# Staging tiles ordered by last use, and a norm started behind the recurrence's last channel

## The chip, the cores and the metric

The kernel runs on one core of one Trainium2 chip. The metric is the device time of one execution in microseconds (us). The core has five engines with an instruction queue each: PE (TensorE, matmuls into PSUM; its weight loads are listed as PEld), DVE (VectorE), ACT (ScalarE), POOL (GpSimd) and SP (SyncE, which here only issues DMAs). Each engine runs its instructions in the order in which they stand; an instruction waits on semaphores of other engines and of DMA queues.

## The reference

Two layers of an encoder, for 2048 prompt frames and 32 further frames of a second request; feature size 1024. Layer 0 is attention (a sliding window branch and a band branch), layer 1 a gated linear recurrence. Each is wrapped in two RMS norms:

```python
hp = rms_norm(yp, ln_pre[l])
...                                   # layer 0
qa, ka, va, ga, qb, kb, vb, gb = ab_project(hp, pos_p, w_in_ab[j])
oa = prompt_band(qa, ka, va, N_PREV_A, None, sinks_a[j])
ob = prompt_band(qb, kb, vb, N_PREV_B, relpos_b[j], None)
mp = concat(oa * silu(ga), ob * silu(gb)) @ w_out
...                                   # layer 1, lru_mixer
xb, z = split(h @ w_in)
xc = conv_b + sum(xp[:, tap:tap + t] * conv_w[tap] for tap in range(4))
r  = sigmoid(xr @ wa + ba);  gi = sigmoid(xr @ wx + bx)
a  = exp(8 * r * log_sigmoid(lam))
u  = sqrt(1 - a * a) * (gi * xc)
h[t] = a[t] * h[t-1] + u[t]
mp = (h * silu(z)) @ w_out
...                                   # both
yp = yp + rms_norm(mp, ln_post[l])
```

The outputs are the two activations, the new key and value caches and the recurrence's states. All is float32.

## The kernel before

**Tiling.** Features lie on the 128 partitions in 8 groups (KT), frames on the free axis. The 2084 frames are cut into six blocks of 352 (the last 324), and worked on in three *thirds* (b = 0, 1, 2) of two blocks (bi = 0, 1). A float32 product is made of three matmuls of a rounded format: every operand is split into a high and a low part (r0h/r0l and r1h/r1l are the two activation tiles, wh/wl the weights), so a block of one result tile is 8 x 3 = 24 matmuls into one PSUM tile (acc, of which there are three from layer 0's out projection on).

**Stages.** Layer 0's in projection for all thirds (`dense_P`) with attention between; then layer 0's out projection of the three thirds (`out_part`); then, for each third, layer 1's in projection with the recurrence (`in_part`, 16 result tiles) and its out projection (`out_part`, 8 result tiles). `dense_2` holds the last two.

**What sets the order.** All engines' instructions are recorded through one helper (line 106 in every profile row), in the order that a small planner (`Sched`) makes: processes are generators that ask for an engine, inputs and buffers; the planner keeps model times and issues from the list by priority. The order is fixed when the program is built; on the chip each engine then keeps it, whatever the true times are. A key set by `sch.set` exists only in the planner. So a process that waits for a key is recorded later, and the chip knows nothing of the key.

**The staging pool and the pool that takes its place.** `sp` (named stg, right side of the memory) holds what layer 0's in projection needs to bring its results out: `s` (seven tiles of 352, the result before it is stored; the gates z are stored from here to `zT` last of all), `sr` (high and low parts), `vst` (transposed values), `xcs` (cosines and sines), `r0b` (a norm's factor). It is closed when layer 0's in projection is recorded, and `mp` takes the same memory: `m` (two tiles of 8 x 352, the out projection's result), `sacc` (sums of squares), `r`, `tz`. Tiles are laid out in the order in which they are made. `reuse_waits="tile"` makes the first write of a tile in `mp` wait for the last use of the tiles that lay in the same place, DMAs that read them included. In `out_part` the first result of a block makes ACT write `m` and `sacc` (`fin_out`, `c == 0`).

**Layer 1.** For a channel group c, `in_part` makes the x branch (`fin_x`): convolution, gates (g, two PSUM tiles, from xs), ACT functions on e and ti, then on DVE `e`, `ti`, the scan over time (the profile's TENSOR_TENSOR_SCAN, `ti<-ex,hcar,ti`), the product with the gate z (ex from tzb), and the split into r0h and r0l. At its end the key `("yc", b, c)` is set. The names ex and eti are tiles that several uses share: ex holds xc, a and sz, and xt at other times; eti holds e or ti.

`out_part` is called with `late=True`: its first two blocks run 21 matmuls each, over the first seven channel groups, and only then the three matmuls each over the eighth, which wait for `("yc", b, 7)`.

**The norm of the next third.** `norm_proc` for third b + 1 is spawned when `in_part` of third b begins. It loads the first block's two halves xt from `x2T`, then for each block: four squares on ACT (sq, one buffer), each followed by a reduction on DVE (ss), their sum, a split into xs, two matmuls with ones on PE (`misc<-xs,onesr`), a square root, reciprocals, products (xt), and the split into r1h and r1l, which the next in projection reads. The second block is loaded into the same tiles when the first is done. With `hold` the process waits for a key before its first square; before, this is `("part", b)`, set when `in_part` of third b has recorded its last matmul.

`sch.alone` keeps POOL out of the choice between DVE and POOL while `in_part` is being recorded; it is set to False when `in_part` ends.

Of the kernel before, what the change touches and what calls it, by code (L numbers as in the profile page):

```python
# [9 lines left out]
F32 = mybir.dt.float32  # L10
F32R = mybir.dt.float32r
# [5 lines left out]
KT = 8  # L17
# [5 lines left out]
BLK = 352  # L23
# [25 lines left out]
PY2, PY3 = 0.5, 3  # L49
# [121 lines left out]
class Sched:  # L171
# [119 lines left out]
    def spawn(self, gen, prio):  # L291
        self.n += 1
        p = [prio, self.n, gen, None]
        p[3] = next(gen, None)
        if p[3] is not None:
            self.procs.append(p)
            self.procs.sort(key=lambda q: (q[0], q[1]))
# [106 lines left out]
def hybrid_kernel(ctx, tc, I, O):  # L404
    nc = tc.nc
    sch = Sched()
# [14 lines left out]
    def ring(pool, shape, tag, bufs, dtype=F32):  # L421
        return Ring(sch, pool, shape, dtype, tag, bufs)
# [189 lines left out]
    hlr = []  # L612
# [131 lines left out]
    r0, fx = [rr_.get(), None], {}  # L744
# [110 lines left out]
    sp = PS.enter_context(tc.tile_pool(name="stg", bufs=1, side="right"))  # L855
# [6 lines left out]
    pS = P.enter_context(tc.tile_pool(name="pS", bufs=1, space=bass.MemoryType.PSUM))  # L862
    pT = P.enter_context(tc.tile_pool(name="pT", bufs=1, space=bass.MemoryType.PSUM))
    pO = P.enter_context(tc.tile_pool(name="pO", bufs=1, space=bass.MemoryType.PSUM))
    sr = ring(sp, [128, BLK], "s", 7)
    srr = ring(sp, [128, 2, BLK], "sr", 3, F32R)
    hlr.append(srr)
    vsr = ring(sp, [128, 3, 2, 128], "vst", 1, F32R)

    xcr = ring(sp, [128, KT, 176], "xcs", 1)  # L870
    xct = {}
    ctn = {}
    r0[1] = sp.tile([128, BLK], F32, name="r0b", tag="r0b")

    def ct_done(b, c):
        n, t = ctn.get((b, c), (0, 0.0))
# [756 lines left out]
    Q = ctx.enter_context(ExitStack())  # L1633
    mp = Q.enter_context(tc.tile_pool(name="mp", bufs=1, side="right", reuse_waits="tile"))
    ac3 = accr
    mr, sar, r2r = ring(mp, [128, KT, BLK], "m", 2), ring(mp, [128, BLK], "sacc", 2), ring(mp, [128, BLK], "r", 1)
    tzr = ring(mp, [128, BLK], "tz", 1)
    sch.cuts.update((x[2].tensor.name, (KT * BLK, BLK // 2)) for x in mr.idle)
    x2n = {}
    gr = []  # L1640
# [214 lines left out]
    def gw_proc():  # L1855

        for b in range(3):
            for c in range(8):
                g, = yield R("SP", rings=[gstr])
                SP.dma_start(out=g, in_=I["gw"][c])  # L1860
                e, (gh, gl) = yield R(("A", "V"), [g], [ghr, glr], cost=(0.3, 0.2))
                if e == "A":
                    A.copy(gh, g)
                else:
                    V.tensor_copy(gh, g)
                e, _ = yield R(("V", "G"), [gh], cost=(0.33, 0.69))
                ENG[e].tensor_tensor(gl, g, f32(gh), OP.subtract)
                gws[(b, c)] = gh, gl
                gstr.release(g)
                sch.set(("gw", b, c), sch.t[e] + 0.13)  # L1870
# [149 lines left out]
    def dense_2():  # L2020
        for b in range(3):
            yield from out_part(b, base + 8 * b, b % 2, I["xT"], LN_POST, x2T, lambda k, bi, b=b: (("y", b), bi), late_m=b > 0)
            if b == 0:

                yield R("PE", [("attention",)])
        spawn(gw_proc(), 1)
        xrr.retire(eti)
        for x in extra:
            xtr.retire(x)
        b1 = base + 24  # L2030
        for b in range(3):
            sch.alone = True
            if b < 2:
                spawn(norm_proc(x2T, b + 1, LN_PRE + 1, 1, (1, b + 1), [xtr, xtr], free=("in", b), src_ready=[("x2", b + 1)],
                                hold=("part", b)), PY3)
            yield from in_part(b, b1 + 24 * b, 1, 0)
            sch.alone = False
            sch.set(("part", b))
            yield from out_part(b, b1 + 24 * b + 16, 0, x2T, LN_POST + 1, O["yT"], lambda k, bi, b=b: ("yc", b, k), late=True, final=b == 2)

    spawn(dense_2(), 9)
    sch.run(lambda: not names() & {"kq_proc", "v_proc", "proc", "reduce"})
    P.close()
# [149 lines left out]
```

## Time and profile before

| what | value |
|---|---|
| median of 3 runs | 1810.09 us (1809.11 to 1812.69) |
| the profiled execution: time, span | 1810.39 us, 1808.6 us |
| PE busy, share of the span | 1726.3 us, 95% |
| DVE, ACT, POOL busy | 1537.9, 1001.9, 322.1 us |
| layer 0's out projection, first third | about 985 to 1053 us |
| layer 1, in projection of the three thirds | 1179 to 1323, 1394 to 1531, 1599 to 1730 us |
| layer 1, out projection of the three thirds | 1323 to 1394, 1531 to 1599, 1730 to 1795 us |

A row of a timeline reads: start in us from the span's start, length in us, engine, line, operation, output <- inputs, shapes, and in brackets how long the engine had been idle and what ended that. A row of stretches gives start and end, length, then for each engine its busy us and the number of instructions, then the granted clock of PE (PEclk, 1.00 is full), the share of time that the DMA engines worked, and GB/s.

### The profile page before, as it was taken

The page shows a single profiled execution, that of the slowest core. Times are in us where ns is not written, and L with a number is a line of the kernel's source. Part 1 is how long each engine was busy: PE and PEld are TensorE (multiplying, and loading weights), DVE is VectorE, ACT ScalarE, POOL GpSimd, SP SyncE. Part 2 cuts the span into 40 slices and gives each one's busy share as a digit, 9 for nine tenths or more (in the row PEclk, how much of TensorE's full clock was granted, in tenths as well). Part 3 has the DMA queues.
Part 4 walks back from the last instruction along what each step waited for, and adds up shares of the span by engine and source line. Part 5 has one row for each costly group of instructions (what it writes and reads, how often), then busy time and mean ns, then how long its engine had stood idle before and what let it go on. Part 6 is the DMA issues. An engine that isn't in the chain of part 4 may idle for free. (4 is left out here: it accounts for less than half of the span.)

```text
span 1808.6 us, 31683 instructions
## 1 busy us (share of the span) xinstructions
PE 1726.3 (95%) x11078; PEld 1674.2 (93%) x11078; DVE 1537.9 (85%) x3228; ACT 1001.9 (55%) x2055; POOL 322.1 (18%) x285
## 2 busy tenths in 40 slices
PE   8998999999999999999997999998989999999997
PEld 7988999898899999899997999998989999999996
DVE  9889977799998769998888689999988998789945
ACT  4275543367766525766664334457754587438742
POOL 4332123322312133323124000000012000100002
PEclk9999999999999999999999999999999999999998
DMA  5787766879565268887875864674556634455466
GB/s 180 204 256 235 227 183 180 225 218 276 161 188 153 73 182 244 209 229 195 226 192 163 274 211 169 233 295 160 207 182 222 246 124 143 162 208 172 146 242 232
DMA packets 232168, 362.80 MB, mean 201 GB/s; under 512 B 36340, under 2 KB 173480, under 8 KB 231992
## 3 DMA queue, kind: packets, MB, share of 16 engines
q1 hardware_dynamic: 232008, 360.78, 64.0%
q8 instruction: 87, 1.43, 0.3%
q14 instruction: 73, 0.60, 0.1%
HBM read 255.77 MB, written 107.00 MB: 201 GB/s over the span
## 5 line engine op out<-in xcount | busy, mean ns | idle before, releaser
L106 PE MATMUL acc<-r0h,wh 128*128 128x352 f32 (+2 forms) x1832 | 592.8, 324 | 11.5 <-ACT r0h L106 10.3
L106 PE MATMUL acc<-r0l,wh 128*128 128x352 f32 (+2 forms) x1832 | 593.1, 324 | 2.1 <-DVE r0l L106 2.0
L106 PE MATMUL acc<-r0h,wl 128*128 128x352 f32 (+2 forms) x1832 | 592.6, 323 | 2.3 <-DMA wl<-wo1s 1.6
L106 PEld LDWEIGHTS acc<-r0h,wh 128*128 128x128 f32 x1832 | 347.1, 189 | 14.0 <-ACT r0h L106 11.2
L106 PEld LDWEIGHTS acc<-r0l,wh 128*128 128x128 f32 x1832 | 347.1, 189 | 4.4 <-DVE r0l L106 3.4
L106 PEld LDWEIGHTS acc<-r0h,wl 128*128 128x128 f32 x1832 | 347.0, 189 | 4.3 <-DMA wl<-wo1s 2.4
L106 PE MATMUL acc<-r1h,wh 128*128 128x352 f32 (+1 forms) x864 | 277.9, 322 | 0.6 <-ACT xb L106 0.6
L106 PE MATMUL acc<-r1h,wl 128*128 128x352 f32 (+1 forms) x864 | 277.7, 321 | 0.0
L106 PE MATMUL acc<-r1l,wh 128*128 128x352 f32 (+1 forms) x864 | 277.6, 321 | 0.0
L106 ACT ACTIVATE pt<-pt,nm 128x256 f32<-128x256 f32 (+6 forms) x272 | 170.3, 629 | 70.0 <-DVE nm L106 68.9
L106 ACT CAST pp<-T 128x256 fp32r<-128x256 f32 (+4 forms) x314 | 133.1, 439 | 74.2 <-PE T L106 62.2
L106 POOL TENSOR_SCALAR pt<-pt,rr 128x256 f32<-128x256 f32 (+5 forms) x144 | 99.3, 699 | 397.5 <-DVE rr L106 183.4
L106 PEld LDWEIGHTS acc<-r1h,wh 128*128 128x128 f32 x864 | 162.7, 188 | 0.9 <-ACT xb L106 0.9
L106 PEld LDWEIGHTS acc<-r1l,wh 128*128 128x128 f32 x864 | 162.8, 188 | 0.0
L106 PEld LDWEIGHTS acc<-r1h,wl 128*128 128x128 f32 x864 | 162.6, 188 | 0.2 <-DVE wl L106 0.2
L106 DVE TENSOR_TENSOR pp<-T,pp 128x256 fp32r<-128x256 f32 (+4 forms) x314 | 151.3, 498 | 8.6 <-ACT pp L106 6.7
L106 PE MATMUL T<-ident,pt 128*128 128x128 f32 (+1 forms) x864 | 141.7, 274 | 15.5 <-DVE pp L106 12.5
L106 PE MATMUL O<-pp,vt 128*128 128x256 f32 (+2 forms) x728 | 133.8, 307 | 8.7 <-DVE pp L106 5.8
L106 PEld LDWEIGHTS T<-ident,pt 128*128 128x128 f32 (+1 forms) x864 | 100.2, 139 | 40.6 <-DVE pp L106 20.0
L106 ACT ACTIVATE m<-acc,vec 128x352 f32<-128x352 f32 (+3 forms) x103 | 51.1, 511 | 141.3 <-PE acc L106 135.6
L106 PE MATMUL S<-kk,qa 128*128 128x320 f32 (+5 forms) x376 | 121.5, 337 | 4.5 <-issue 1.5
L106 PEld LDWEIGHTS O<-pp,vt 128*128 128x128 f32 x728 | 104.5, 189 | 13.0 <-DVE pp L106 7.1
(243 smaller groups left out, 3051.6 us busy)
## 6 DMA issues: line engine op xcount, KB each, us to landing
wst<-w_in SPq DMA_DIRECT2D x93, 512.0 KB, 4.9
wst<-wo_in SPq DMA_DIRECT2D x32, 512.0 KB, 4.1
wh<-w1s SPq DMA_DIRECT2D x32, 512.0 KB, 3.6
wl<-w1s SPq DMA_DIRECT2D x32, 512.0 KB, 4.8
wh<-wo1s SPq DMA_DIRECT2D x24, 512.0 KB, 3.8
wl<-wo1s SPq DMA_DIRECT2D x24, 512.0 KB, 4.7
kk<-kB SPq DMA_DIRECT2D x32, 320.0 KB, 4.9
vt<-vB SPq DMA_DIRECT2D x16, 640.0 KB, 4.7
```

The costliest lines, as they stand in the source:

```text
L106: r = fn(*a, **k)
```

## The change

Three edits. The tiles of `sp` are made in the order r0b, vst, xcs, sr, s instead of s, sr, vst, xcs, r0b. The tiles of `mp` are made in the order sacc, r, tz, m instead of m, sacc, r, tz. The next third's norm waits for `("yc", b, 7)`, whose model time is the end of the eighth channel's split, instead of `("part", b)`.

```diff
-    sr = ring(sp, [128, BLK], "s", 7)
+
+    r0[1] = sp.tile([128, BLK], F32, name="r0b", tag="r0b")
+    vsr = ring(sp, [128, 3, 2, 128], "vst", 1, F32R)
+
+    xcr = ring(sp, [128, KT, 176], "xcs", 1)
     srr = ring(sp, [128, 2, BLK], "sr", 3, F32R)
     hlr.append(srr)
-    vsr = ring(sp, [128, 3, 2, 128], "vst", 1, F32R)
-
-    xcr = ring(sp, [128, KT, 176], "xcs", 1)
+    sr = ring(sp, [128, BLK], "s", 7)
     xct = {}
     ctn = {}
-    r0[1] = sp.tile([128, BLK], F32, name="r0b", tag="r0b")
...
-    mr, sar, r2r = ring(mp, [128, KT, BLK], "m", 2), ring(mp, [128, BLK], "sacc", 2), ring(mp, [128, BLK], "r", 1)
+
+    sar, r2r = ring(mp, [128, BLK], "sacc", 2), ring(mp, [128, BLK], "r", 1)
     tzr = ring(mp, [128, BLK], "tz", 1)
+    mr = ring(mp, [128, KT, BLK], "m", 2)
...
                 spawn(norm_proc(x2T, b + 1, LN_PRE + 1, 1, (1, b + 1), [xtr, xtr], free=("in", b), src_ready=[("x2", b + 1)],
-                                hold=("part", b)), PY3)
+                                hold=("yc", b, KT - 1)), PY3)
             yield from in_part(b, b1 + 24 * b, 1, 0)
             sch.alone = False
-            sch.set(("part", b))
```

By bytes, the first `m` (bi = 0) lay over all seven `s` and the first `sr`, and lies now over `xcs` and `sr`; the second (bi = 1) lies now over `sr` and the seven `s`.

What the planner makes of it. Up to the end of layer 1's first in projection every engine has the same instructions in the same order; only waits differ. ACT's rows at the first result of layer 0's out projection, before (m is the result's tile, acc its PSUM tile, the numbers are buffers, and each DMAHW is a semaphore of DMA queues):

```order
L106 CAST r0h<-xr_153 128x4x176 [waits Pool_49]
L106 ACTIVATE m_10500<-acc_158,vec 128x2x176 [waits DMAHW2_49,DMAHW1_49,DMAHW3_49,DMAHW0_49,DMAHW6_49,DVE_49,PE_49]
L106 ACTIVATE sacc_10502<-acc_158 128x352
L106 CAST r0h<-xt_151 128x4x176 [waits DVE_49]
L106 CAST r0h<-xt_152 128x4x176 [waits DVE_49]
L106 CAST r1h<-ex_0_10570 128x4x176 [waits DMAHW4_49,DVE_49]
L106 CAST wh_119<-wst_118 128x1024 [waits DMAHW5_49,PE_49]
L106 ACTIVATE m_10501<-acc_0_10557,vec 128x2x176 [waits PE_49]
```

The same rows of ACT now:

```order
L106 CAST r0h<-xr_153 128x4x176 [waits Pool_49]
L106 ACTIVATE m_10504<-acc_158,vec 128x2x176 [waits DVE_49,PE_49]
L106 ACTIVATE sacc_10500<-acc_158 128x352
L106 CAST r0h<-xt_151 128x4x176 [waits DVE_49]
L106 CAST r0h<-xt_152 128x4x176 [waits DVE_49]
L106 CAST r1h<-ex_0_10570 128x4x176 [waits DMAHW2_49,DMAHW3_49,DMAHW1_49,DMAHW4_49,DMAHW0_49,DVE_49]
L106 CAST wh_119<-wst_118 128x1024 [waits DMAHW5_49,PE_49]
L106 ACTIVATE m_10505<-acc_0_10557,vec 128x2x176 [waits DMAHW2_49,DMAHW3_49,DMAHW1_49,DMAHW6_49,DMAHW0_49,PE_49]
```

Nothing moved; the waits on DMAs went from the first m to the r1h cast and the second m.

DVE at the end of layer 1's first in projection, before. These are the eighth channel's e, ti, scan (here SCALAR_TENSOR_TENSOR `ti<-ex,hcar,ti`), the product with the gate, and r0l, with the norm's reductions (ss) and the out projection's weights (wl) among them:

```order
L106 SCALAR_TENSOR_TENSOR e_10562<-ex_0_10571,e_10562 128x704
L106 TENSOR_REDUCE ss_155<-sq_154 128x176
L106 TENSOR_TENSOR ti_10563<-ti_10563,e_10562 128x704
L106 TENSOR_TENSOR wl_122<-wst_117,wh_119 128x1024
L106 SCALAR_TENSOR_TENSOR ti_10563<-ex_0_10571,hcar,ti_10563 128x704
L106 COPY hcar<-ti_10563 128x1
L106 SCALAR_TENSOR_TENSOR ex_0_10571<-tzb_10558,acc_159 128x352
L106 TENSOR_REDUCE ss_156<-sq_154 128x176
L106 SCALAR_TENSOR_TENSOR ti_10563<-ti_10563,ex_0_10571 128x704
L106 TENSOR_REDUCE ss_155<-sq_154 128x176
L106 TENSOR_TENSOR r0l<-ti_10563,r0h 128x704
L106 TENSOR_REDUCE ss_156<-sq_154 128x176
```

The same place on DVE now:

```order
L106 SCALAR_TENSOR_TENSOR e_10562<-ex_0_10571,e_10562 128x704
L106 TENSOR_TENSOR ti_10563<-ti_10563,e_10562 128x704
L106 SCALAR_TENSOR_TENSOR ti_10563<-ex_0_10571,hcar,ti_10563 128x704
L106 COPY hcar<-ti_10563 128x1
L106 SCALAR_TENSOR_TENSOR ex_0_10571<-tzb_10558,acc_159 128x352
L106 SCALAR_TENSOR_TENSOR ti_10563<-ti_10563,ex_0_10571 128x704
L106 CAST r0h<-ti_10563 128x704
L106 TENSOR_TENSOR r0l<-ti_10563,r0h 128x704
L106 TENSOR_REDUCE ss_155<-sq_154 128x176
L106 CAST wh_120<-wst_118 128x1024
```

Three reductions moved behind r0l, the cast r0h came over from ACT, and wl went to POOL, whose rows from there on are, now:

```order
L106 TENSOR_TENSOR wl_124<-wst_117,wh_121 128x1024
L106 TENSOR_TENSOR wl_122<-wst_117,wh_119 128x1024
L106 TENSOR_TENSOR sacc_10501<-sacc_10501,tzb_10558 128x352
L106 TENSOR_TENSOR wl_122<-wst_118,wh_119 128x1024
L106 TENSOR_TENSOR sacc_10500<-sacc_10500,tz_10503 128x352
```

The second of these is the wl that moved; POOL's row ahead of it is from layer 0's out projection. On ACT the first square of this norm now stands behind the weights' cast and the gate's tzb, the others behind the evacuation of the first two blocks. On PE the norm's two matmuls (misc) stand 32 matmuls later.

DVE at the end of the second in projection, before:

```order
L106 TENSOR_TENSOR ti_10563<-ti_10563,e_10562 128x704
L106 TENSOR_REDUCE ss_155<-sq_154 128x176
L106 SCALAR_TENSOR_TENSOR ti_10563<-ex_0_10571,hcar,ti_10563 128x704
L106 COPY hcar<-ti_10563 128x1
L106 SCALAR_TENSOR_TENSOR ex_0_10571<-tzb_10558,acc_159 128x352
L106 TENSOR_REDUCE ss_156<-sq_154 128x176
L106 SCALAR_TENSOR_TENSOR ti_10563<-ti_10563,ex_0_10571 128x704
L106 TENSOR_REDUCE ss_155<-sq_154 128x176
L106 TENSOR_TENSOR r0l<-ti_10563,r0h 128x704
L106 TENSOR_REDUCE ss_156<-sq_154 128x176
```

And now:

```order
L106 TENSOR_TENSOR ti_10563<-ti_10563,e_10562 128x704
L106 SCALAR_TENSOR_TENSOR ti_10563<-ex_0_10571,hcar,ti_10563 128x704
L106 COPY hcar<-ti_10563 128x1
L106 SCALAR_TENSOR_TENSOR ex_0_10571<-tzb_10558,acc_159 128x352
L106 SCALAR_TENSOR_TENSOR ti_10563<-ti_10563,ex_0_10571 128x704
L106 CAST r0h<-ti_10563 128x704
L106 TENSOR_TENSOR r0l<-ti_10563,r0h 128x704
L106 TENSOR_REDUCE ss_155<-sq_154 128x176
```

Again the reductions moved behind r0l and the cast came to DVE; no weights are split in between. ACT has two of the four squares ahead of the first evacuation and two behind the second block's. On PE the norm's two matmuls stand 36 matmuls later, and the sum of the two ss halves (`ss<-ss,ss`) is on POOL. From there on the third in projection has its instructions in a somewhat different order: the gates' matmuls stand 8 to 16 matmuls later.

## The prediction

> **What bounds the kernel now.** I read the page first, then the waits of PE, then the time around its longest waits.
>
> ```profile
> span 1808.6 us, 31683 instructions
> ...
> PE 1726.3 (95%) x11078; PEld 1674.2 (93%) x11078; DVE 1537.9 (85%) x3228; ACT 1001.9 (55%) x2055; POOL 322.1 (18%) x285
> ```
>
> PE is the bound: only what shortens PE's stream or its waits shortens the kernel. The waits of PE, by what ended them (total us, times, longest):
>
> ```profile
> PE acc L106 <- ACT r0h L106: 10.3, 3, 4.6
> ...
> PE acc L106 <- DVE r0l L106: 2.0, 3, 1.0
> ```
>
> These six are three pairs at three places, which I call A (988 us: first result of layer 0's out projection), B0 and B1 (1330 and 1538 us: layer 1's out projection of the first and the second third, two blocks in, where the eighth channel is needed). In the stretches below, the columns are length, then busy us and instructions of PE, PEld, DVE and ACT, then PEclk, the granted clock.
>
> ```profile
> 984.80:988.01 3.21, 3.21 (x20) 2.92 (x19) 3.13 (x5) 0.65 (x1) 2.47 (x1) 1.00 0.94 282
> 988.01:992.62 4.61, 0.00 (x0) 0.00 (x1) 0.02 (x1) 1.57 (x3) 2.12 (x1) 0.94 0.55 139
> 992.62:998.94 6.32, 6.05 (x19) 5.68 (x20) 3.59 (x5) 1.56 (x2) 0.00 (x0) 0.51 1.02 309
> 1329.77:1333.83 4.06, 0.17 (x2) 0.00 (x0) 3.91 (x6) 1.52 (x2) 0.00 (x0) 0.94 0.71 234
> 1333.83:1340.35 6.52, 5.71 (x19) 5.34 (x19) 5.39 (x5) 2.96 (x6) 2.75 (x2) 0.51 0.20 79
> 1538.23:1540.22 1.99, 0.16 (x2) 0.00 (x0) 1.93 (x3) 1.57 (x2) 0.00 (x0) 1.00 0.00 0
> 1540.22:1545.17 4.95, 3.97 (x13) 3.73 (x14) 4.14 (x6) 3.33 (x6) 0.00 (x0) 0.66 0.20 16
> ```
>
> At full speed 20 matmuls take 3.21 us, 0.16 each. After each wait the clock is halved for some 3.4 or 6.8 us. So A costs 4.61 + 6.32 - 19 x 0.16 = 7.9 us; B0 costs 4.06 + 6.52 - 18 x 0.16 = 7.7 (18 begin in it); B1 costs 1.99 + 4.95 - 13 x 0.16 = 4.9. Together 20.5 us can be had. The rest of PE's waits the change leaves alone.
>
> **A: the tiles in another order.** The queue, ACT, DVE and POOL around 988 us; the first row is the issue line of the last store from a staging tile (median us to landing last).
>
> ```profile
> zT<-s SPq DMA_DIRECT2D x1, 162.0 KB, 5.3
> ...
> 985.44 0.46 SPq L106 DMA_DIRECT2D zT<-s  x1
> ...
> 985.54 4.60 POOL L106 TENSOR_TENSOR wl<-wst,wh 128x1024 fp32r<-128x1024 f32 x1 [3.68 <-DVE wh L106]
> ...
> 987.05 0.88 DVE L106 TENSOR_TENSOR xt<-xt 128x704 f32<-128x704 f32 x1
> ...
> 990.99 0.56 ACT L106 ACTIVATE m<-acc,vec 128x352 f32<-128x352 f32 x1 [5.54 <-DMA xt<-zT]
> 991.45 0.46 ACT L106 ACTIVATE sacc<-acc 128x352 f32<-128x352 f32 x1
> 991.79 0.78 ACT L106 CAST r0h<-xt 128x704 fp32r<-128x704 f32 x1
> ...
> 992.60 0.89 DVE L106 TENSOR_TENSOR r0l<-xt,r0h 128x704 fp32r<-128x704 f32 x1 [4.67 <-ACT r0h L106]
> ```
>
> The store is issued at 985.44 and lands 5.3 later, at 990.8 (the profile names another transfer of the same moment, the load xt<-zT; m waits for five DMA semaphores); m, whose tile lies over its source, is written at 990.99, 3 us after its matmuls ended (988.01). Behind m in ACT's order stands the r0h cast that PE waits for. In the changed order m's wait names no DMA any more; the first m lies over tiles last used earlier. Then m runs at 988.25 (0.25 for the signal, an estimate from 990.8 to 990.99), r0h 0.80 behind it, at 989.05, its input ready since 987.93; PE restarts at 989.9 instead of 992.62. The next step is late at once: r0l has to share with POOL, which works on wl until 990.13, so it ends at 991.05. The second piece (xt 0.88, r0h 0.78, r0l 0.89) ends at 993.55; before, PE at half clock hid it, now PE waits 0.8 us more for it. The 20 steps from the last matmul before the wait end at 994.55 instead of 998.94: 4.4 us. If the clock halves once, it is 3.3. I take 3.8. Ends: 2.0 (halved twice) and 5. The second m, which now lies over the late tiles, is written some 9 us later, after the store has landed: nothing. The r1h cast behind takes over the DMA waits, but is needed only 50 us later: nothing. The tiles' new places cost no instruction.
>
> **B0: the norm's squares behind the eighth channel.** ACT and DVE in the order of the chain that ends at r0h and r0l:
>
> ```profile
> 1324.38 0.78 ACT L106 ACTIVATE sq<-xt 128x704 f32<-128x704 f32 x1
> 1325.06 1.03 ACT L106 CAST wh<-wst 128x1024 fp32r<-128x1024 f32 x1
> ...
> 1333.00 0.78 ACT L106 CAST r0h<-ti 128x704 fp32r<-128x704 f32 x1
> ```
> ```profile
> 1324.50 0.89 DVE L106 SCALAR_TENSOR_TENSOR e<-ex,e 128x704 f32<-128x704 f32 x1
> 1325.31 1.46 DVE L106 TENSOR_REDUCE ss<-sq 128x176 f32<-128x704 f32 x1
> 1326.69 0.88 DVE L106 TENSOR_TENSOR ti<-ti,e 128x704 f32<-128x704 f32 x1
> 1327.49 1.22 DVE L106 TENSOR_TENSOR wl<-wst,wh 128x1024 fp32r<-128x1024 f32 x1
> 1328.62 1.68 DVE L106 TENSOR_TENSOR_SCAN ti<-ex,hcar,ti 128x704 f32<-128x704 f32 x1
> ...
> 1330.40 0.51 DVE L106 SCALAR_TENSOR_TENSOR ex<-tzb,acc 128x352 f32<-128x352 f32 x1
> 1330.83 1.33 DVE L106 TENSOR_REDUCE ss<-sq 128x176 f32<-128x704 f32 x1
> 1332.09 0.88 DVE L106 SCALAR_TENSOR_TENSOR ti<-ti,ex 128x704 f32<-128x704 f32 x1
> ...
> 1334.35 0.89 DVE L106 TENSOR_TENSOR r0l<-ti,r0h 128x704 fp32r<-128x704 f32 x1
> ```
>
> The changed order takes three reductions out from between e and r0l, gives wl to POOL and the r0h cast to DVE. What those cost, by the nearest rows: the cast on DVE, and a DVE addition without and with POOL at work.
>
> ```profile
> 1223.00 0.52 DVE L106 CAST r0h<-eti 128x704 fp32r<-128x704 f32 x1
> ```
> ```profile
> 1351.38 0.52 DVE L106 TENSOR_TENSOR sacc<-sacc,tz 128x352 f32<-128x352 f32 x1
> ...
> 1357.77 2.02 DVE L106 TENSOR_TENSOR sacc<-sacc,tzb 128x352 f32<-128x352 f32 x1
> ```
> ```profile
> 1357.61 1.81 POOL L106 TENSOR_TENSOR r1l<-xt,r1h 128x704 fp32r<-128x704 f32 x1
> ```
>
> The addition waits until POOL is done (1359.42) and ends 0.4 behind it. Now: ti runs 1325.4 to 1326.3; without the square, wh is cast at 1324.6 (its load landed) to 1325.7, and POOL asks for wl then, before the scan does. A wl alone on POOL lasts some 2.2 us (4.60 less DVE's work to 987.93 in A's row), so POOL holds to 1328.5 and the scan ends at 1330.05, hardly sooner than the 1330.30 of before. The two moves eat each other up there. Behind the scan ex, ti, r0h (0.52) and r0l give r0h at 1332.1 and r0l at 1333.0. PE goes on at 1332.2 and 1333.1 instead of 1333.83 and 1335.30; 17 more matmuls bring it to 1335.8, where it was at 1340.35: 4.55, less 1.5 if the clock still halves, which 2.4 us of waiting do about as often as not. One thing more: the norm's remaining squares and reductions now run after r0l and alternate with ACT's evacuations; PE meets the norm's sum 32 matmuls later in its order, and by the same durations its input is ready 0.5 us after PE gets there. I take 3.5. The low end is 2.0 (POOL holds up two instructions of the chain instead of one), the high end 6.0 (it holds up none: scan to 1328.0, r0l 1331.0).
>
> The Trainium skill, "SBUF — State Buffer", section "Who interferes with whom", says that a DVE instruction with two SBUF inputs and a GpSimd one that reads SBUF exclude each other, and that the one issued first keeps the ports for its whole length; the scan has two such inputs, and no row here shows one beside POOL. By it the term is 3.5, and 6.0 were the scan exempt. It speaks against this part of the change.
>
> **B1.** Here no wl stands in the chain. Rows of the two reductions in it, and of the cast:
>
> ```profile
> 1533.59 1.42 DVE L106 TENSOR_REDUCE ss<-sq 128x176 f32<-128x704 f32 x1
> ...
> 1537.14 1.41 DVE L106 TENSOR_REDUCE ss<-sq 128x176 f32<-128x704 f32 x1
> ```
> ```profile
> 1539.39 0.78 ACT L106 CAST r0h<-ti 128x704 fp32r<-128x704 f32 x1
> ```
>
> r0h was ready at 1540.17; less 1.3 for each reduction (they overlap their neighbours by 0.1) and 0.26 for the cast it is ready at 1537.4, r0l at 1538.4. PE needs them at 1538.23 and 1538.39: all 4.9 us come back. But the norm's sum: four reductions (1.4) with squares (0.78) between and four evacuations (1.8) among them, from 1538.4, then the addition on POOL (0.94, by the row of its like below) and two halves of a split (0.9) end at 1548.8. PE gets to that sum 36 matmuls later in its order than before, at 1539.2 + 48 x 0.16 = 1546.9. It waits 1.9 us. Net 2.9 to 3.0; ends 1.0 and 4.9. I take 2.9.
>
> ```profile
> 1336.76 0.94 POOL L106 TENSOR_TENSOR ss<-ss,ss 128x352 f32<-128x352 f32 x1 [346.63 <-DVE ss L106]
> ```
>
> **What moves on the queue.** The load of the next third's second half (xt<-x2T) stands ahead of two weight stores after B0 and behind two weight loads after B1. PE needs its result only at the next in projection, so I put it at 0; the slower rival below prices it.
>
> **The last third** has its gate matmuls 8 to 16 matmuls later in PE's order and some casts on another engine. No wait of PE over 0.4 us stands in its stretch, and at its end ACT's row of work is one instruction shorter: 0, ends -1 and +1.
>
> **Sum.** 3.8 + 3.5 + 2.9 = 10.2 us. The profiled execution took 1810.39 (its span and 1.8 around it), the median of the three runs is 1810.09, so 1810.1 - 10.2 = 1799.9.
>
> **Rivals.**
> - *The clock stays full at A and B0.* Both new waits, 1.9 and 2.4 us and each followed by one of 0.7 to 1.0, are about as long as B1's 1.99, in which PE was busy for 0.16 us and after which the mean clock was 0.66; If they fall across two of the clock's windows it stays full: A gives 4.4 and B0 4.0, in all 11.3, so 1798.8. Chance 0.10. The Trainium skill, "TensorE: Matmul & The Clock Gate", section "What's actually happening", lets the clock halve only after an idle window of about 3.4 us; by that rule this rival would hold. The trace disagrees at B1, where a wait of 1.99 us was enough.
> - *The scan is not held up by POOL* (POOL asks after it, or yields as in A's row, where it took 4.60): B0 gives 6.0, 1797.4. Chance 0.18.
> - *The gain is given back later*: sums and in projections wait for the later norm, and half of it stays, 1805. Chance 0.10.
> - *A does not happen*: the r0h cast finds another late input, 1803.7. Against it: ACT's order shows only DVE there. Chance 0.06.
> - *Slower: the norm is late for the next in projection.* Its last r1l is just in time for the second block of it (26 matmuls after 1394.38, so 1398.5):
>
> ```profile
> 1396.16 0.89 DVE L106 TENSOR_TENSOR r1l<-xt,r1h 128x704 fp32r<-128x704 f32 x1
> ```
> If the norm is one serial chain, starting it 8.7 us later (first square 1324.38, now behind r0l at 1333.0) puts this r1l at 1405.8, and PE, 3.5 sooner, wants it at 1395.0: it waits 10.8 us, and then at half clock for 3.4 more. 14.2 - 10.2: 1814. Decides from 10.2 us of lateness. Against it: in the old trace the norm itself waits for ACT and the queue, its second half is reloaded after the first, and that load now stands ahead of two stores. Chance 0.06.
>
> My forecast has the remaining 0.50. A measurement of this kernel can tell 0.2%, 3.6 us. Low end: B0 uncontended, B1 whole, A at 4.4: 1794.9. High end: 2.0 + 2.0 + 1.0: 1805.1. So 1795 to 1805. Faster 0.88, same 0.06, slower 0.06.
>
> **What would show it.** A right: m no longer starts behind a DMA, and PE's wait there is 2 us or less. B0: r0h comes from DVE and a scan of 3 us or more beside POOL's wl; a scan of 1.7 means the first rival. B1: no wait for r0h, one of about 2 us for the norm's sum (misc<-xs). The prediction falls if PE waits for r1h or r1l at the start of an in projection.

## The result, and the profile after

The changed kernel takes 1799.56 us (median of 6 runs, 1798.55 to 1802.74), the kernel before 1810.79 beside it: ratio 0.9936, 95% interval 0.9923 to 0.9948. The forecast was 1799.9, in a range of 1795 to 1805.

The page of the changed kernel, its first line and the busy times:

```profile
span 1800.9 us, 31686 instructions
...
PE 1725.7 (96%) x11078; PEld 1672.7 (93%) x11078; DVE 1536.2 (85%) x3224; ACT 1000.2 (56%) x2058; POOL 325.5 (18%) x286
```

PE's busy time is what it was; waits have gone. The waits of PE that name r0h, r0l or the norm's sum (total us, times, longest):

```profile
PE acc L106 <- DVE r0h L106: 2.7, 1, 2.7
PE misc L106 <- DVE xs L106: 2.6, 2, 1.4
...
PE acc L106 <- ACT r0h L106: 1.7, 1, 1.7
...
PE acc L106 <- DVE r0l L106: 1.4, 2, 0.9
```

Before, r0h and r0l cost 12.3 us in six waits; now 5.8 in four. One of 1.7 and one of 0.9 are A, one of 2.7 and one of 0.5 are B0, and B1 has none of them left; it has a new one of 1.2 for the norm's sum, the shorter of the two for xs (the other was there before). The stretches that answer to those of before (length; busy us and instructions of PE, PEld, DVE, ACT, POOL; granted clock; DMA):

```profile
987.70:992.64 4.94, 3.28 (x21) 2.99 (x19) 3.25 (x7) 2.31 (x5) 4.10 (x1) 1.00 0.87 267
992.64:994.85 2.21, 1.32 (x6) 1.08 (x7) 2.06 (x2) 0.11 (x1) 0.51 (x1) 1.00 0.41 71
994.85:998.34 3.49, 3.49 (x15) 3.49 (x14) 0.89 (x1) 0.67 (x1) 0.00 (x0) 0.51 0.92 290
1328.95:1331.66 2.71, 0.00 (x1) 0.00 (x0) 2.57 (x6) 0.00 (x0) 0.00 (x0) 1.00 0.98 310
1331.66:1336.20 4.54, 4.04 (x14) 3.80 (x15) 4.25 (x5) 2.46 (x5) 0.00 (x0) 0.62 0.24 95
1534.00:1536.00 2.00, 1.92 (x12) 1.63 (x12) 1.97 (x3) 0.00 (x0) 0.00 (x0) 1.00 0.00 0
```

At A and at B0 the clock still halves, once each for some 3.4 us; where B1's waits for r0h and r0l stood, PE now works at full clock (the last row). Around A, engine by engine (start, duration, and in brackets the idle time before and what ended it):

```profile
988.45 0.46 SPq L106 DMA_DIRECT2D zT<-s  x1
988.54 4.61 POOL L106 TENSOR_TENSOR wl<-wst,wh 128x1024 fp32r<-128x1024 f32 x1 [3.68 <-DVE wh L106]
...
991.02 0.55 ACT L106 ACTIVATE m<-acc,vec 128x352 f32<-128x352 f32 x1 [2.58 <-PE acc L106]
...
991.81 0.78 ACT L106 CAST r0h<-xt 128x704 fp32r<-128x704 f32 x1
...
992.62 1.28 DVE L106 TENSOR_TENSOR r0l<-xt,r0h 128x704 fp32r<-128x704 f32 x1 [1.69 <-ACT r0h L106]
992.64 0.42 PE L106 MATMUL acc<-r0h,wh 128*128 128x352 f32 x1 [1.66 <-ACT r0h L106]
...
993.96 0.43 PE L106 MATMUL acc<-r0l,wh 128*128 128x352 f32 x1 [0.89 <-DVE r0l L106]
```

m starts behind its matmul and no longer behind a transfer: the store is issued at 988.45 and m is written at 991.02, before a store of 5.3 us could have landed. r0l takes 1.28 instead of 0.89 beside POOL's wl. Around B0:

```profile
1325.43 2.60 POOL L106 TENSOR_TENSOR wl<-wst,wh 128x1024 fp32r<-128x1024 f32 x1 [332.28 <-ACT wh L106]
...
1325.80 3.71 DVE L106 TENSOR_TENSOR_SCAN ti<-ex,hcar,ti 128x704 f32<-128x704 f32 x1
...
1331.09 0.53 DVE L106 CAST r0h<-ti 128x704 fp32r<-128x704 f32 x1
...
1331.66 0.43 PE L106 MATMUL acc<-r0h,wh 128*128 128x352 f32 x1 [2.71 <-DVE r0h L106]
```

The scan, 1.68 us elsewhere, takes 3.71: it ends 1.48 us after POOL's wl (1328.03), so nearly all of it seems to have run behind that instruction; run 5 tests this.

**A finer measure than the span.** The profiled pair differs by 7.7 us in its spans, the medians by 11.2. Most of the 3.5 us between the two is in code that no part of the change touches: it took 3.2 us longer in the changed kernel's profile (column "start to A" below). I cut each profile at the same places in PE's order and took the time from first matmul to first matmul: from the start of the projections to 21 matmuls ahead of A's wait; from there over the next 481 matmuls, which end a quarter into the second third of layer 0's out projection (A; the expectations below call this the stretch from A to the end of the out projection, but it stops at 1069 us in the profile before, and that projection goes on to 1179); layer 1's out projection of the first third (B0), its in projection of the second third, and its out projection of the second third (B1). "Clock lost" is what halved windows cost in the first stretch.

| kernel | median us | start to A | of it clock lost | A | out, 1st third | in, 2nd third | out, 2nd third |
|---|---|---|---|---|---|---|---|
| before | 1810.79 | 948.7 | 1.7 | 84.74 | 71.48 | 137.16 | 67.56 |
| changed | 1799.56 | 951.9 | 5.1 | 81.31 | 67.55 | 138.28 | 64.18 |
| changed, again | 1799.65 | 948.6 | 3.4 | 81.24 | 67.52 | 137.48 | 64.39 |
| tiles alone | 1805.88 | 947.8 | 5.1 | 80.34 | 70.22 | 138.00 | 66.24 |
| staging tiles alone | 1805.75 | 946.9 | 1.7 | 82.23 | 71.75 | 137.00 | 68.31 |
| result tiles alone | 1808.18 | 945.3 | 1.8 | 82.23 | 70.89 | 136.97 | 68.35 |
| hold alone | 1801.16 | 944.2 | 3.5 | 83.91 | 67.45 | 136.54 | 64.12 |
| wl after r0l | 1797.52 | 950.2 | 5.1 | 81.24 | 65.77 | 136.79 | 64.12 |
| the same, sum later | 1795.04 | 946.7 | 1.7 | 82.15 | 65.45 | 136.41 | 63.12 |
| the same, again | 1797.26 | 949.9 | 5.1 | 80.30 | 65.49 | 136.83 | 63.13 |
| norm 4 us later | 1815.9 | 946.5 | 3.4 | 80.29 | 68.23 | 156.04 | 64.14 |
| norm 8 us later | 1837.88 | 947.4 | 3.5 | 81.41 | 66.91 | 155.80 | 64.95 |
| 8 us later, norm first | 1803.73 | 946.4 | 1.7 | 81.44 | 69.91 | 139.74 | 65.17 |

The first stretch has one instruction order and varies by 7.8 us, so a single span says little about a change of 10; the stretches behind it vary by up to 2.1 us among kernels that have the same order there (B1 with the old hold: 66.24 to 68.35). By the pair before and changed the change gives 3.4 at A, 3.9 at B0 and 3.4 at B1, 10.7 in all. Against the other kernels with the old hold B0 gives 2.7 to 4.2 and B1 2.1 to 4.2. Of B1's 3.4, 0.3 are only a matter of counting: two matmuls of a norm's sum that ended this stretch before now stand behind its end, in the third in projection.

### The profile page after: what moved, and what is told of

Same layout as the page of the kernel before. It is cut to its first block, busy times and chain, and to the rows that moved or that the text cites. A ratio compares the mean times of both kernels' runs of the same rounds, so it can differ in the third digit from the quotient of the medians.

```text
span 1800.9 us, 31686 instructions
## 1 busy us (share of the span) xinstructions
PE 1725.7 (96%) x11078; PEld 1672.7 (93%) x11078; DVE 1536.2 (85%) x3224; ACT 1000.2 (56%) x2058; POOL 325.5 (18%) x286
## 4 chain that ended last, share of the span: by engine, by line
PE 58%; DVE 24%; DMA 6%; ACT 6%; issue 4%; SPq 1%; POOL 0%; DVEq 0%; ACTq 0%; POOLq 0%
PE acc L106 44%; PE O L106 4%; PE S L106 4%; PE T L106 4%; DVE pt L106 3%; DVE ss L106 2%; DVE ex L106 2%; DVE pp L106 2%; DVE m L106 2%; PE g L106 2%; DVE s L106 2%; DVE ti L106 1%; DVE ot L106 1%; DVE wl L106 1%; DVE r0l L106 1%
## 5 line engine op out<-in xcount | busy, mean ns | idle before, releaser
L106 POOL TENSOR_TENSOR wl<-wst,wh 128x1024 fp32r<-128x1024 f32 x40 | 99.7, 2494 | 441.5 <-ACT wh L106 398.6
```

Of the source, the lines that this page charges most:

```text
L106: r = fn(*a, **k)
```

## The experiments

The kernel before took 1810.02, 1809.74, 1808.66 and 1810.15 us beside the four groups of runs that follow.

**1. The tiles alone.** The hold of the norm stays as before:

```
-                                hold=("yc", b, KT - 1)), PY3)
+                                hold=("part", b)), PY3)
```


> The tiles and the out projection's results in the new order, the hold of the norm as before. My theory: A is worth 3.4 us by itself, in any company, so 1807.4 us (1806.5 to 1808.5); m waits for no DMA, PE's waits at A are 1.7 and 0.9 us, B0 and B1 stand as before (4.1 us and 2.0 us waits). Rival 1: the places of tiles matter elsewhere too, or the gain at A only comes together with the other change: under 1.5 us or over 5 us. Rival 2: the clock halves twice at A by chance of its window: 1809.

1805.88 us, ratio 0.9982 (0.9970 to 0.9994), below my 1806.5. PE's waits at A are 1.67 and 0.87 us as in the changed kernel. But the clock stayed full behind them in this profile:

```profile
986.40:989.40 3.00, 0.47 (x2) 0.22 (x2) 1.36 (x2) 1.57 (x3) 2.16 (x1) 1.00 0.57 191
989.40:993.00 3.60, 3.24 (x19) 2.96 (x20) 1.60 (x2) 0.78 (x1) 0.00 (x0) 1.00 0.86 256
```

So A gave 4.4 here (84.74 to 80.34), the value that the prediction had for a full clock, and 3.4 where it halved. The same two waits do either; the last section shows on what it hangs. B0 and B1, which this kernel leaves as they were, took 1.3 us less each than in the profile before (70.22 and 66.24), with PE's first wait there 3.9 and 2.0 us long as expected; in each of the two stretches halving cost 1.7 us less.

**2. The hold alone.** The tiles stay as before, the norm is held behind the eighth channel.

> The hold of the norm behind the eighth channel alone, tiles as before. My theory: B0 gives 3.9 and B1 3.4, the in projection behind B0 takes back 1.1, so -6.2 in the stretches and some 1.0 less than all three terms together: 1804.0 us (1803 to 1805.5). PE's wait at A is as before, 4.6 us. Rival: the parts are not additive, since an in projection hides what comes late: the hold alone gives under 4 us (above 1806.8) or over 8 us (below 1802.8).

1801.16 us, ratio 0.9963 (0.9946 to 0.9980); 1.8 below the low end of what I expected, and by the time (8.9 us) in the range of the rival. The stretches do not bear the rival's reason out: the out projections took 67.45 and 64.12 us, just as with the whole change, 4.0 and 3.4 less than before, and A 83.91. The in projection behind B0 took 136.54, so the 1.1 us that I had put down to the change (138.28 against 137.16) are not its cost: the tiles alone, with the old hold, had 138.00. The stretch ahead of A was the shortest of all profiles (944.2). The two halves give 4.1 and 8.9 us by the medians, 13.0 against 11.2 and 9.0 in the two measurements of the whole; with 95% intervals of some 2 to 3 us either way that neither shows an interplay of a few us nor excludes one.

**3. The staging tiles alone**, m, sacc, r and tz in the old order.

> Only the staging tiles in the new order; the out projection's m, sacc, r, tz in the old order, and the hold as before. By the order the first m now waits for DVE and PE and for no DMA, the second m for three DMA semaphores. Theory 1: what counts at A is that the first m waits for no store; then this gives A whole, -3.4 us (1807.4), and the new order of m, sacc, r, tz is worth nothing. Theory 2: both orders are needed, because sacc or tz now lies over what is stored last: a wait of ACT for a DMA behind m, a gain under 1.5 us (1809.3 or more).

1805.75 us, ratio 0.9980 (0.9968 to 0.9991): as much as both orders together. m starts behind its matmul, and PE waits as in the changed kernel:

```profile
986.44 0.55 ACT L106 ACTIVATE m<-acc,vec 128x352 f32<-128x352 f32 x1 [4.14 <-PE acc L106]
...
988.06 0.43 PE L106 MATMUL acc<-r0h,wh 128*128 128x352 f32 x1 [1.66 <-ACT r0h L106]
```

So theory 1 holds: this order alone takes the store out of the way. The stretch fell only to 82.23, since in this profile the clock was halved ahead of A, when PE came late anyhow; the kernel with the hold alone had the same, and there, with the store, it was 83.91:

```profile
986.08 0.55 ACT L106 ACTIVATE m<-acc,vec 128x352 f32<-128x352 f32 x1 [5.72 <-DMA xt<-zT]
...
987.71 0.43 PE L106 MATMUL acc<-r0h,wh 128*128 128x352 f32 x1 [3.25 <-ACT r0h L106]
```

Between these two A gives 1.7 us, half of what it gives where PE arrives at full clock.

**4. The order of the result's tiles alone**, staging tiles as before.

> Only the out projection's tiles in the new order (sacc, r, tz, m), the staging tiles in the old one and the hold as before. By the order the first m now waits for two DMA semaphores where it waited for five, and for DVE and PE. Theory 1: what counts is the store that lands last, and it is still among the two: m starts behind a store as before, the stretch from A to the end of the out projection takes 84 to 85 us as before, time 1809 to 1811. Theory 2: the last store is not among the two: the stretch takes 80 to 82.5 us as with the staging tiles in the new order, time 1806 us.

1808.18 us, ratio 0.9993 (0.9980 to 1.0005): not to be told from before. By its length, 82.23, the stretch would fit theory 2, but the profile shows a case that neither theory had:

```profile
986.02 0.55 ACT L106 ACTIVATE m<-acc,vec 128x352 f32<-128x352 f32 x1 [4.13 <-PE acc L106]
987.29 0.46 ACT L106 ACTIVATE sacc<-acc 128x352 f32<-128x352 f32 x1 [0.72 <-DMA zT<-s]
...
988.48 0.42 PE L106 MATMUL acc<-r0h,wh 128*128 128x352 f32 x1 [2.49 <-ACT r0h L106]
```

m is free of the store, but sacc behind it now lies over the stored tile and waits for it, with r0h behind both in ACT's order. The wait has moved one instruction on. PE waits 2.49 us, between the 3.25 and the 1.66 of the two kernels whose clock was halved ahead of A as it was here. The length of the stretch owes to the clock: halving cost 1.6 us in it, 3.4 with the staging tiles alone and 3.3 with the hold alone. Less that, it is 80.6 as with the hold alone, and 78.8 with the staging tiles alone.

**5. wl away from the scan.** At B0 the low half of the third result's weights is recorded behind the eighth channel:

```
-            e, _ = yield R(("V", "G"), [h], cost=(1.14, 2.3))
+            e, _ = yield R(("V", "G"), [h, ("yc", 0, KT - 1)] if WSEQ[i] == ("wo1", 2) else [h], cost=(1.14, 2.3))
```


> The changed kernel with one difference: at B0 the low half of the third result's weights (wl) is recorded behind the eighth channel's split, so DVE makes it after r0l and POOL has nothing there. Theory 1: POOL's wl holds the scan up by 2.0 us (3.71 instead of 1.68). Then the scan takes 1.7, PE's first wait at B0 falls from 2.71 to about 0.7, its clock loses less or nothing, and the time is 1797.5 us (1796.5 to 1798.5), -2.0 against the changed kernel. Theory 2: the scan is slow for another reason, or PE then waits for r0l or for the weights instead: the scan still takes over 3 us, or the time is 1799.5 +-0.7.

1797.52 us, ratio 0.9930 (0.9914 to 0.9947). DVE makes it behind r0l, POOL has nothing there, and the scan takes 1.69:

```profile
1324.62 1.69 DVE L106 TENSOR_TENSOR_SCAN ti<-ex,hcar,ti 128x704 f32<-128x704 f32 x1
...
1328.46 0.43 PE L106 MATMUL acc<-r0h,wh 128*128 128x352 f32 x1 [0.69 <-DVE r0h L106]
1329.25 1.22 DVE L106 TENSOR_TENSOR wl<-wst,wh 128x1024 fp32r<-128x1024 f32 x1
...
1340.92 0.99 PE L106 MATMUL misc<-xs,onesr 128*128 128x352 f32 x2 [0.91 <-ACT xs L106]
```

POOL's wl was what held the scan up. The first 80 matmuls of the stretch take 14.48 us, 18.08 in the changed kernel: 3.6 us, 2.0 of them the wait and the rest the clock, which stays full. The stretch as a whole gains 1.8, mainly since PE now comes to the norm's sum 0.9 us too soon: the lead falls by 1.6 us over the sum's two matmuls. In "SBUF — State Buffer", section "Who interferes with whom", the Trainium skill lets a DVE instruction with two SBUF inputs and a GpSimd one that reads SBUF keep each other out until the first is done; the 3.71 and the 1.69 agree with it for the scan.

**6. The norm's sum later.** On top of run 5, PE's matmuls of the norm's sum at B1 are recorded 1.0 us later, 8 matmuls further back in its order:

```
+        tx = sch.w[t.tensor.name] + late
-        ps, = yield R("PE", [t], [psr_])
+        ps, = yield R("PE", [lambda: tx], [psr_])
...
-            ps = yield from norm_sum(sa[:, :tot])
+            ps = yield from norm_sum(sa[:, :tot], 1.0 if key == (1, 2) and bi == 0 else 0.0)
```


> The changed kernel with the third result's wl made by DVE behind r0l at B0, and PE's matmuls of the norm's sum at B1 recorded 1.0 us later, which puts them some 9 matmuls further back. My theory: PE's wait of 1.2 us for the norm's sum goes, since those matmuls fill it, and nothing waits for the sum instead: the stretch of the out projection's second third falls from 64.1 to 62.9 us, that of the first third to 65.8 us as in the run before this, the time is 1796.5 us (1795 to 1798), -3 against the changed kernel. Rival: the norm's end is needed at the next in projection and PE waits there instead: 64.1 us or a longer in projection, 1797.5 us or more.

1795.04 us, ratio 0.9923 (0.9909 to 0.9938). The sum's matmuls run without a wait,

```profile
1536.64 0.99 PE L106 MATMUL misc<-xs,onesr 128*128 128x352 f32 x2
```

the stretch falls from 64.12 to 63.12, and the in projection behind it is no longer. Once more beside the changed kernel:

> The changed kernel once more, on the chip of the run behind it. 1799.5 us (1797 to 1802). If A, B0 and B1 are what moved, the stretches from A, of the out projection's first and second third take 80.3 to 82.3, 67.5 and 64.2 us, and the in projection behind B0 136.5 to 138.3 us, its length no matter of the change; if the change costs it something, 138 us or more again.

> The kernel with wl behind r0l at B0 and the norm's sum later at B1, once more beside the changed kernel on one chip. My theory: 3 us below it (2 to 4.5): 1796.3 us. Rival: its 1795.0 was the chip, and it stands within 1.5 us of the changed kernel.

1799.65 us (ratio 0.9946, 0.9930 to 0.9962) and 1797.26 (0.9932, 0.9918 to 0.9947). In the stretches of this pair, B0 and B1, the second kernel is 2.0 and 1.3 us quicker, 3.3 together, as expected; the medians differ by 2.4 and the intervals overlap, so as a time this is likely and not shown. By its medians it is the quickest kernel of the study.

**7. The norm later still.** The hold is moved 8 us further back:

```
-                                hold=("yc", b, KT - 1)), PY3)
+                                hold=lambda b=b: None if ("yc", b, KT - 1) not in sch.key else sch.key["yc", b, KT - 1] + 8.0), PY3)
```


> The changed kernel with the norm of the next third held 8 us more behind the eighth channel's split. Now the last low half (r1l) ends 2.7 us after the in projection's start in the second third and 0.4 us before it in the last third; PE needs it 3.9 us after the start (24 matmuls). Theory 1 (the slower rival of the prediction: the norm is one serial chain, so 8 us later is 8 us later at its end): PE waits 8 - 1.2 = 6.8 us in the second third and 8 - 4.3 = 3.7 us in the last, and some 1.7 us of half clock behind each: 1799.6 + 14 = 1813 us (1809 to 1815). Theory 2 (its end is set by other things, the reload of its second half and ACT's evacuations, since the end in the second third stood 2.7 us after the in projection's start both before and after the change): PE waits under 4 us in all, 1800 to 1805 us.

1837.88 us, ratio 1.0151 (1.0135 to 1.0168): both theories wrong by far. Twice PE waits for r1h:

```profile
PE acc L106 <- ACT r1h L106: 33.0, 2, 16.7
```

DVE's row there, and ACT's cast that waits for it:

```profile
1383.54 3.27 DVE L106 SCALAR_TENSOR_TENSOR xt<-xt,vec,ss 128x176 f32<-128x176 f32 x8
...
1390.07 1.68 DVE L106 TENSOR_TENSOR m<-m,r 128x880 f32<-128x880 f32 x2
...
1404.57 1.33 DVE L106 SCALAR_TENSOR_TENSOR xt<-xt,vec,ss 128x176 f32<-128x176 f32 x4
...
1405.93 1.37 ACT L106 CAST r1h<-xt 128x1408 fp32r<-128x1408 f32 x1 [8.57 <-DVE xt L106]
```

The norm's last multiplications come behind the out projection's own norm (m<-m,r, m<-m,xr, from 1390.07 on), and with them r1h. In the changed kernel all of them stand ahead of it:

```profile
1383.69 5.00 DVE L106 SCALAR_TENSOR_TENSOR xt<-xt,vec,ss 128x176 f32<-128x176 f32 x8
...
1394.22 1.68 DVE L106 TENSOR_TENSOR m<-m,r 128x880 f32<-128x880 f32 x2
```

With 4 us:

> As the run with 8 us, but the norm held 4 us more. In the run with 8 us PE waited 16.7 and 16.3 us for r1h, because the last multiplications of the norm (xt<-xt,vec,ss) came behind a row of some 12 us of DVE's work on the out projection's own norm (m<-m,r and m<-m,xr). Theory 1 (a cliff: either the norm gets past that row or it stands behind it): with 4 us in the second third the same as with 8, a wait of 10 us or more for r1h at one in projection at least, 1808 us or more. Theory 2 (the cost grows in step with the lateness): half of the cost, waits of some 8 us each, 1816 to 1822 us at both. Theory 3 (4 us fit in the slack): 1799 to 1803 us.

1815.9 us, ratio 1.0045 (1.0030 to 1.0059): the same 16.7 us once, in the second third, and none in the last. It is a cliff, and in the second third its edge is within 4 us of the changed kernel in the planner's time. On the chip, counted from the out projection's first matmul, the norm's first square came at 13.1 us there, at 17.2 with 8 us and at 4.9 in the changed kernel. To see whether the place in DVE's row does it, the 8 us again with a priority of 0 instead of 3 for the norm:

```
-PY2, PY3 = 0.5, 3
+PY2, PY3 = 0.5, 0
```


> The run with the norm held 8 us more, with one number changed besides: the norm's priority for the planner (PY3) is 0 instead of 3, so by the order all its multiplications and splits stand ahead of the out projection's own norm (m<-m,r) in DVE's row, in the second third and in the last. It starts as late as there. Theory 1 (the 16.7 us are the place in DVE's row, not the 8 us): the waits for r1h are gone or under 4 us each, the two in projections take 136.5 to 141 and 131 to 134 us, the time is 1798 to 1806 us. Theory 2 (the lateness itself): the waits stay over 8 us, over 1820 us.

1803.73 us, ratio 0.9975 (0.9960 to 0.9990). The norm is as late as in the run with 8 us (first square 17.5 us after the out projection's first matmul, 17.2 there; last 57.9 and 58.0), and the waits for r1h are gone:

```profile
1385.20 3.28 DVE L106 SCALAR_TENSOR_TENSOR xt<-xt,vec,ss 128x176 f32<-128x176 f32 x8
1388.40 1.68 DVE L106 TENSOR_TENSOR r1l<-xt,r1h 128x704 fp32r<-128x704 f32 x2
...
1394.39 1.69 DVE L106 TENSOR_TENSOR m<-m,r 128x880 f32<-128x880 f32 x2
```

So 34 of the 38 us go with the place in the row (the priority may move other work too). Of the other 4, 2.1 are longer waits for the norm's sums, 2.6 us in the changed kernel and here

```profile
PE misc L106 <- DVE xs L106: 4.7, 5, 1.4
```

## Why the prediction was right, point by point

- **Sum.** 10.2 us forecast; the stretches give 10.7 (10.4 over the same matmuls), the medians 11.2 and 9.0. The three mechanisms are the ones named.
- **A, 3.8.** Measured 3.4 with one halving and 4.4 with none; the working had 3.3 and 4.4. PE's waits were 1.66 and 0.89 us where the working had 1.9 and about 1.0. What it left out is that PE may come to A with its clock already halved; then the store has less to hold up, and A gives 1.7. Of the two orders the staging tiles' does it alone.
- **B0, 3.5.** Measured 3.9, by a route that is partly luck. In the first 80 matmuls, where the working put all of it, the stretch gains 2.6 (20.64 to 18.08; 0.3 of it are the sum's two matmuls, which now come later); halved once, the working gave 4.55 - 1.5 = 3.05 there. The other 1.4 are later in the stretch, and 0.9 of them are a wait that the old order had at the second half's sum and the new one hasn't, as the row before and the row after show:

```profile
1381.25 0.99 PE L106 MATMUL misc<-xs,onesr 128*128 128x352 f32 x2 [0.93 <-ACT xs L106]
```
```profile
1376.80 0.94 PE L106 MATMUL misc<-xs,onesr 128*128 128x352 f32 x2
```

  The loss of 0.5 at the first half's sum, which the working took off, did not come; it came in run 5, where PE was sooner. The scan beside POOL came as priced (end at 1329.51 against 1330.05), and the 6.0 without POOL stand against 71.48 - 65.77 = 5.7.
- **B1, 2.9.** Measured 3.4, or 3.1 over the same number of matmuls. All of the waits for r0h came back, as worked out, but for the 0.08 that r0l is late; the new wait for the sum is 1.20 and not 1.9. The chain from r0l on is as long as worked out, but PE starts with the high half of the sum, which the working had not used: the cast that makes it ends at 1544.87, and the low half comes beside PE's first matmul.

```profile
1544.53 0.34 DVE L106 CAST xs<-ss 128x352 fp32r<-128x352 f32 x1 [0.82 <-POOL ss L106]
...
1544.93 0.99 PE L106 MATMUL misc<-xs,onesr 128*128 128x352 f32 x2 [1.20 <-DVE xs L106]
```

- **In projections, queue and last third, 0.** Right within what the profiles vary.
- **The rivals.** The clock staying full at A is what some runs do and others don't, for the reason that this rival gave (last section), so it was no case of its own but a term of 1 us either way. The scan not held up by POOL: refuted by the changed kernel's scan of 3.71 us and by run 5. The slower rival is where the working was wrong. It took the norm for one serial chain that becomes late from 10.2 us on and costs as much as it is late. It also put the first square behind r0l; on the chip that square came at 4.9 us after the out projection's first matmul, 1.5 before, and the first reduction, which does stand behind r0l, at 10.3 against 2.4. Yet the last square of the norm came at 51.2 us, 54.9 before: the start does not set the end. Its end in the second third stood 2.7 us after the in projection's start before the change and after it (1397.05 against 1394.38, 1392.34 against 1389.66), and its cost is a step of 16.7 us at an edge less than 4 us of hold away, set by what stands ahead of it in DVE's row. The change did not reach the edge, but its chance was not read from the row that decides it.

## What to carry to other kernels

When work is moved back behind a critical chain, ask what else is queued on the engine that will do it: the price is not how much later it starts but which row it ends up behind. When two stages share memory, follow the chain of every instruction ahead of the critical one on its engine; freeing one tile can move the wait to the next. And cut the profiles at the same instruction of the bound engine before comparing them: here such stretches repeated to about 2 us where the code ahead of them varied by 8.

## What the runs showed of the hardware

The granted clock halves in pieces of 3.41 us (or multiples) that fall in other places in each run of one instruction order. In the stretch ahead of A, which varies by 7.8 us, they cost 1.7 to 5.1 us. PE's waits there vary too, from 29.5 to 35.2 us in all; less both, the stretch is 911.1 to 912.9 us long in every profile. Waits of 1.67 and 0.87 us (tiles alone) left the clock full, waits of 1.66 and 0.89 us (changed kernel) halved it for one such piece:

```profile
994.85:998.26 3.41, 3.41 (x14) 3.41 (x13) 0.89 (x1) 0.67 (x1) 0.00 (x0) 0.50 0.91 289
```

Where the pieces begin tells why. Within one profile all of them begin on one grid of 3.41 us, and the grid lies elsewhere in each run. In the changed kernel most of the first wait (1.2 us) and all of the second fall into one piece of it, in which PE was busy for 1.34 us, and the next piece is halved. With the tiles alone the grid cuts through the first wait, 1.2 us ahead of the cut and 0.5 behind it together with the second wait, and PE was busy for 2.21 and 2.08 us of the two pieces. These are the piece of the changed kernel and the two with the tiles alone:

```profile
991.46:994.87 3.41, 1.34 (x7) 1.10 (x8) 2.08 (x2) 1.26 (x4) 1.69 (x1) 1.00 0.53 134
```
```profile
984.18:987.59 3.41, 2.21 (x14) 1.92 (x13) 2.17 (x4) 1.16 (x3) 3.41 (x1) 1.00 0.88 244
987.59:991.01 3.42, 2.08 (x11) 1.83 (x12) 2.12 (x3) 1.20 (x2) 0.97 (x1) 1.00 0.50 130
```

Counted like this over the thirteen profiles of the table, from 25 to 1780 us of each, the clock went from full to half 66 times, each time behind a piece in which PE had been idle for at least 1.56 us; of some 6500 pieces that left it full none had PE idle for more than 1.88 us.

The Trainium skill, "TensorE: Matmul & The Clock Gate", section "What's actually happening", has the half clock after an idle window of about 3.4 us. The length of the pieces agrees; that PE must have been idle for all of one does not, since it was idle for 2.07 us of the 3.41 ahead of the halving shown.
